# Seven products per gate/up side and per down projection: which PSUM bank each adds into, which engine reads it, and in what order

## The chip, the cores and the metric

One core of a Trainium2 chip runs the program. The time is device time in microseconds of one execution of the whole layer; the runs of before took 1701.79 us in the median of three (1700.83 to 1703.76). TensorE (PE) multiplies matrices and adds the results in PSUM; ScalarE (ACT), VectorE (DVE) and GpSimd (POOL) do elementwise work; SyncE (SP) issues the transfers. Each engine works through a queue of its own in order and waits there for what an instruction needs.

## What is computed

One layer of a sequence model for 1024 tokens of width 1024 in float32: a gated feed-forward network (FFN), a mixer (a gated convolution beside a state space model) and a second FFN. The changed code serves the two FFNs:

```python
def swiglu(h, w_gate, w_up, w_down):
    return (jax.nn.silu(h @ w_gate) * (h @ w_up)) @ w_down
...
h = modulate(rms_norm(x, ffn1_norm[l]), sh1, sc1)
x = x + 0.5 * g1[:, None, :] * swiglu(h, ffn1_w_gate[l], ffn1_w_up[l], ffn1_w_down[l])
```

The FFN is 2816 wide.

## The kernel before

**Products.** A float32 product is made of three matmuls (`mm3`): each operand is split into a high part of the type fp32r and a low part, and high x high, high x low and low x high are added up in PSUM. The FFN's width is cut into 11 groups of 256, called fa0 to fa10 in the first FFN and fb0 to fb10 in the second. In most of them (fa2 to fa10 and fb1 to fb10, 19 groups) gate and up are each a product of 2 x 2 blocks made of seven block products instead of eight (`seven`, from line 649). One block product is 12 matmuls. The blocks of the activations on the left are A11, A12, A22 and four combinations S1 to S4. The weights on the right have combinations as well: t1 to t4 beside chunks 0, 2 and 3. Each side, gate (g) and up (u), gives four results: (0,0), (0,1), (1,0) and (1,1). The results of gate pass through silu, those of up are multiplied by them. Most groups keep these products for the down projection (`keep`), and make their sums S1, S2, S3 (`keep_sums`) and S4 (`keep_last`) at once.

**Banks.** A product adds into a PSUM tile of its side: fa6gC is bank C of the gate side of group fa6. Before, the order on a side is A11 into A, S1 into C, S2 into B, S3 into D, A12 into A, A22 into E, S4 into C: five banks. ScalarE copies bank A after A11 (tile t, shown as fa6gt), before A12 adds to it. VectorE adds: u2 = t1 + B, u3 = u2 + D, t1 = u3 + C, u3 = u3 + E, u2 = u2 + C; u2 and u3 are shown as fa6gu. S4 adds to bank C after VectorE has read it for t1 = u3 + C.

**Down projections.** Four calls of `down7` (line 735), fad_0 and fad_1 in the first FFN (lines 1434 and on) and fbd_0 and fbd_1 in the second, use the same scheme with two pieces for each block product, in the order A11, S2, A12, S3, S1, A22, S4 (banks A, B, A, B, C, B, C). Each result goes into x with one VectorE operation (`update`).

**Weights.** The class `Weights` (line 121) feeds them. SyncE loads raw tiles (two slots). GpSimd makes f = chunk 2 - chunk 1 (line 168, in a tile `sums`, two slots) and t1 (line 169), later t2 = f + chunk 0 (line 177) and t4 = chunk 3 - t2 (line 179). ScalarE casts a chunk to the high part (CAST), VectorE subtracts for the low part. Two chunks make a granule, which serves two products; there are three slots `w` for granules.

**What sets the order.** The code calls the engines in the order of the products; side work (the rotors and tables of the state space model: `rott`, `kc`, `mi`, `rt`, `tab`, `kk`, `ph`, `pd`) is let in by a clock that counts products. But outside the first part of the program the framework's scheduler orders each engine's queue, so which instruction stands behind which is seen in the order of the built program, not in the code.

Of the kernel before, what the change touches and what calls it, by code (L numbers as in the profile page):

```python
# [13 lines left out]
F32 = mybir.dt.float32  # L14
# [7 lines left out]
P = 128  # L22
# [98 lines left out]
class Weights:  # L121
# [5 lines left out]
    SEVEN = (0, "t1", "t2", "t3", 3, "t4", 2)  # L127
    SECOND = (0, "t2", 3, "t3", "t1", "t4", 2)

    def __init__(self, engines, srcs, granules, raw_bufs):  # L130
# [4 lines left out]
        for pair in granules:  # L135
            for j, _ in pair:
                self.left[j] += 1
# [26 lines left out]
    def combine(self, j):  # L164
# [5 lines left out]
        self.sums[j] = {"t1": r[1], "t2": r[0], "t3": f, "t4": r[0]}  # L170

    def split_done(self, j, c):

        if j in self.combined and c in (0, "t2"):
            s, r = self.sums[j], self.raws[j][:, :HALF]
            if c == 0:
                self.G.tensor_tensor(out=r, in0=s["t3"], in1=r, op=ALU.add)  # L177
            else:
                self.G.tensor_tensor(out=r, in0=self.chunk(j, 3), in1=r, op=ALU.subtract)  # L179
# [6 lines left out]
    def pump(self):  # L186
        while self.slots and len(self.tiles) < len(self.granules):
# [22 lines left out]
            for j, _ in pair:  # L210
                self.left[j] -= 1
# [24 lines left out]
def hymba_layer(ctx: ExitStack, tc, x_d, xt_d, wm1_d, wmod_d, gu1_d, gs1_d, ds1_d, wl1_d, win_d, wout_d, glu_d, gu2_d, gs2_d, wd2_d, ds2_d, wl2_d, cols_d, cond_d, lam_d, bc_d, out_d):  # L236
# [54 lines left out]
    def stream(gu, gs, wd, ds, wl, m):  # L291
# [4 lines left out]
        for g in range(m, NGRP):  # L296
# [3 lines left out]
            seven = [(i, c) for i in (j, j + 1 + inner) for c in Weights.SEVEN]  # L300
# [5 lines left out]
        for c in range(CHUNKS):  # L306
            for p in range(2):
                j = len(srcs)
                srcs.extend([ds[c, p, 0], ds[c, p, 1]])
                granules.extend([(j, s), (j + 1, s)] for s in Weights.SECOND)  # L310
# [334 lines left out]

    SEVEN = (("A11", "A"), ("S1", "C"), ("S2", "B"), ("S3", "D"), ("A12", "A"), ("A22", "E"), ("S4", "C"))
    SECOND = (("A11", "A"), ("S2", "B"), ("A12", "A"), ("S3", "B"), ("S1", "C"), ("A22", "B"), ("S4", "C"))

    def seven(name, between, place=1, kept=None, then=None):


        a_tiles, gate_, taken = {}, {}, []

        for side in "gu":
            bank, res = {}, {}

            def add(dst, src, b):
                V.tensor_tensor(out=dst[:], in0=src[:], in1=bank[b][:], op=ALU.add)

            def out(h, fi, t):  # L660
                nm = f"{name}_{fi}_{h}"
                if side == "g":
                    A.activation(t[:], t[:], AF.Silu)
                    gate_[h, fi] = t
                elif kept is None:
                    V.tensor_tensor(out=t[:], in0=t[:], in1=gate_[h, fi][:], op=ALU.mult)
                    a_tiles[fi, h] = split_act(t[:], nm + "a")
                else:
                    keep(kept, f"A{h + 1}{fi + 1}", t[:], gate_[h, fi][:], ALU.mult, name, t[:])

            for n, (left, b) in enumerate(SEVEN):
                q = n + 7 * (side == "u")
                if q % 2 == 0:
                    taken = ws.take()
                opens = b not in bank
                if opens:
                    bank[b] = ps(f"{name}{side}{b}")
                for k in range(4):
                    while len(blocks[left]) <= k:
                        clock.step()  # L680
                    mm3(bank[b][:], taken[0], q % 2 * 4 + k, blocks[left][k], opens and k == 0, k == 3, more=not opens)
                nm = f"{name}{side}"
                if n == 0:
                    t1 = t2k(nm + "t1")
                    A.copy(t1[:], bank["A"][:])
                elif n == 2:
                    u2 = t2k(nm + "u2")
                    add(u2, t1, "B")
                elif n == 3:
                    u3 = t2k(nm + "u3")  # L690
                    add(u3, u2, "D")
# [1207 lines left out]
```

## Time and profile before

| | |
|---|---|
| time, median of three runs | 1701.79 us (1700.83 to 1703.76) |
| span of the profiled execution | 1704.7 us |
| mean granted TensorE clock | 0.994 |
| TensorE matmuls | 1666.8 us busy, 7545 instructions |
| VectorE | 1255.5 us busy |
| ScalarE | 630.1 us busy |
| GpSimd | 382.0 us busy |

The first FFN takes up about the first third of the span, the mixer the second, the second FFN the last. A profile row such as `fa2gC<-h1S,w` names the tile that is written and those that are read; `[0.93 <-DVE fa2gt]` behind a row is the time that the engine was idle just before it, and the engine and the tile that ended that. In a list of waits the columns are the total in us, how often, and the longest.

### The profile page before, as it was taken

What the parts mean: (1) busy time and instruction counts of PE and PEld (TensorE: products, weight loads), DVE (VectorE), ACT (ScalarE), POOL (GpSimd) and SP (SyncE); (2) the same over time, 40 slices, a digit from 0 to 9 for tenths busy, and PEclk for the clock granted to TensorE, in tenths of its full rate; (3) what the DMA queues carried; (4) which work ended last, traced back from release to release, by engine and by line L of the source; (5) the groups of instructions that cost most, each with busy time, mean ns of one, the idle gap of its engine ahead of it and who ended that gap; (6) DMA issues with size and microseconds to landing.
All of it is one profiled execution on the core that took longest, in us unless ns stands there. A gap on an engine that the chain in (4) does not pass through costs nothing.

```text
span 1704.7 us, 20844 instructions
## 1 busy us (share of the span) xinstructions
PE 1666.8 (98%) x7545; PEld 1369.9 (80%) x7545; DVE 1255.5 (74%) x1957; ACT 630.1 (37%) x1064; POOL 382.0 (22%) x297
## 2 busy tenths in 40 slices
PE   8999999999999999999999999999999999999997
PEld 5888877788878888788777878888888888888886
DVE  7897899998589978735555857957767667576655
ACT  6525323333354332331113415434344434322233
POOL 1012222242222412100000021122333223333212
PEclk9999999999999999999999999999999999999999
DMA  8544454544665448244654232324443343759212
GB/s 350 187 148 137 172 189 155 183 149 139 213 216 170 151 152 291 70 111 149 191 151 134 70 129 112 112 74 182 188 174 148 148 173 148 269 228 381 110 50 99
DMA packets 101625, 281.48 MB, mean 165 GB/s; under 512 B 19345, under 2 KB 34961, under 8 KB 90386
## 3 DMA queue, kind: packets, MB, share of 16 engines
q1 hardware_dynamic: 101522, 280.15, 46.6%
q8 instruction: 59, 0.97, 0.2%
q14 instruction: 44, 0.36, 0.1%
HBM read 195.69 MB, written 76.02 MB: 159 GB/s over the span
## 4 chain that ended last, share of the span: by engine, by line
PE 70%; DVE 8%; DMA 5%; issue 1%; ACT 0%; SPq 0%; POOL 0%; DVEq 0%; ACTq 0%; POOLq 0%
PE wo L112 4%; PE fald L112 3%; PE fb10d L112 2%; PE u L112 2%; PE fbd_1B L112 2%; PE fbd_0B L112 2%; DMA swz<-si 2%; DVE w L112 2%; PE fad_1B L112 2%; PE b L112 2%; PE fad_0B L112 1%; PE c L112 1%; PE fb0u L112 1%; PE fad_1C L112 1%; PE fbd_1C L112 1%; PE fbd_0C L112 1%
## 5 line engine op out<-in xcount | busy, mean ns | idle before, releaser
L112 ACT CAST w<-raw 128x512 fp32r<-128x512 f32 (+1 forms) x374 | 240.9, 677 | 497.7 <-issue 72.7
L112 DVE TENSOR_TENSOR w<-raw,w 128x512 fp32r<-128x512 f32 (+1 forms) x374 | 311.2, 851 | 101.2 <-ACT w L112 100.6
L177 POOL TENSOR_TENSOR raw<-sums,raw 128x512 f32<-128x512 f32 x54 | 81.6, 1511 | 420.9 <-DVE w L112 419.9
L168 POOL TENSOR_TENSOR sums<-raw 128x512 f32<-128x512 f32 x54 | 76.4, 1415 | 308.1 <-DMA raw<-in_ds 129.1
L179 POOL TENSOR_TENSOR raw<-raw 128x512 f32<-128x512 f32 x54 | 82.3, 1526 | 86.6 <-DVE w L112 86.0
L112 DVE CUSTOM_DVE_ANT_0 wm<-wm,cact 128x1024 f32<-128x1024 f32 x56 | 77.7, 1407 | 15.1 <-DMA wm<-in_wmod 15.0
L169 POOL TENSOR_TENSOR raw<-raw 128x512 f32<-128x512 f32 x54 | 85.2, 1577 | 4.2
L370 POOL TENSOR_TENSOR n3aq<-n3aq,n3aq 128x512 f32<-128x512 f32 x5 | 7.5, 1499 | 277.4 <-ACT n3aq L112 277.2
L112 DVE TENSOR_TENSOR w<-sums,w 128x512 fp32r<-128x512 f32 x54 | 54.9, 1029 | 3.4 <-ACT w L112 2.8
L112 PE MATMUL p<-h,w 128*128 128x512 f32 x192 | 49.4, 407 | 2.0 <-ACT h L112 1.5
L112 PE MATMUL wo<-oa,w 128*128 128x512 f32 x192 | 45.5, 391 | 2.1 <-ACT w L112 1.3
L112 PE MATMUL c<-h,w 128*128 128x512 f32 x192 | 47.1, 397 | 0.0
L112 PE MATMUL v<-h,w 128*128 128x512 f32 x192 | 46.9, 395 | 0.0
L112 PE MATMUL b<-h,w 128*128 128x512 f32 x192 | 45.6, 393 | 0.0
L112 PE MATMUL wo<-ob,w 128*128 128x512 f32 x192 | 45.2, 391 | 0.0
L112 PE MATMUL u<-h,w 128*128 128x512 f32 x192 | 44.8, 392 | 0.2 <-DVE h L112 0.2
L112 PEld LDWEIGHTS wo<-oa,w 128*128 128x128 f32 x192 | 35.8, 188 | 10.2 <-ACT w L112 1.7
L112 PEld LDWEIGHTS p<-h,w 128*128 128x128 f32 x192 | 35.7, 192 | 10.1 <-ACT h L112 2.0
L112 ACT CAST w<-sums 128x512 fp32r<-128x512 f32 x54 | 32.7, 619 | 28.8 <-PE fa10gE L112 2.5
L112 PEld LDWEIGHTS u<-h,w 128*128 128x128 f32 x192 | 35.7, 188 | 8.3 <-DVE h L112 0.6
L112 PEld LDWEIGHTS wo<-ob,w 128*128 128x128 f32 x192 | 35.8, 188 | 7.4
L112 PEld LDWEIGHTS c<-h,w 128*128 128x128 f32 x192 | 35.8, 190 | 7.2
(1579 smaller groups left out, 4039.8 us busy)
## 6 DMA issues: line engine op xcount, KB each, us to landing
raw<-in_gs SPq DMA_DIRECT2D x38, 1024.0 KB, 5.0
wm<-in_wmod SPq DMA_DIRECT2D x56, 512.0 KB, 5.2
raw<-in_ds SPq DMA_DIRECT2D x16, 1024.0 KB, 6.6
mw<-in_wm SPq DMA_DIRECT2D x8, 1024.0 KB, 8.4
raw<-in_win SPq DMA_DIRECT2D x8, 1024.0 KB, 5.5
raw<-in_gu SPq DMA_DIRECT2D x6, 1024.0 KB, 4.9
raw<-in_wl SPq DMA_DIRECT2D x5, 1024.0 KB, 6.7
xb<-in_xt SPq DMA_DIRECT2D x8, 512.0 KB, 6.4
```

The source lines that it names most:

```text
L112: r = getattr(self.engine, name)(*args, **kw)
L168: self.G.tensor_tensor(out=f, in0=r[2], in1=r[1], op=ALU.subtract)
L169: self.G.tensor_tensor(out=r[1], in0=r[1], in1=r[0], op=ALU.subtract)
L177: self.G.tensor_tensor(out=r, in0=s["t3"], in1=r, op=ALU.add)
L179: self.G.tensor_tensor(out=r, in0=self.chunk(j, 3), in1=r, op=ALU.subtract)
L370: nc.gpsimd.tensor_tensor(out=a, in0=a, in1=sq[:, :n], op=ALU.add)
```

## The change

Each side now has six products: A11 into B, S1 into C, S2 into B, A12 into A, S3 into B, S4 into C. Bank B carries A11, A11 + S2 and A11 + S2 + S3 in turn. ScalarE copies it after A11 (t1) and after S2 (u2), and copies bank C after S1 (c1). VectorE adds t1 + A for the result (0,0), c1 + B for (1,1) and u2 + C for (0,1). After both sides come the two A22 products, one adding to bank B of gate, one to bank B of up, and the result (1,0) is read straight from these banks. `down7` follows the same order, with A22 last. The granules of the weights follow: the two t4 form one at the group's end; t4 now lies in the tile `sums` instead of the raw tile, and a raw tile counts as free before t4 is used. `keep_sums` and `keep_last` both come behind the second A22. The tiles and products of the mixer stay as they were.

```diff
-    SEVEN = (0, "t1", "t2", "t3", 3, "t4", 2)
-    SECOND = (0, "t2", 3, "t3", "t1", "t4", 2)
+    SIX = (0, "t1", "t2", 3, "t3", 2)
+    ALL = (*SIX, "t4")
...
-            for j, _ in pair:
-                self.left[j] += 1
+            for j, c in pair:
+                self.left[j] += c != "t4"
...
-        self.sums[j] = {"t1": r[1], "t2": r[0], "t3": f, "t4": r[0]}
+        self.sums[j] = {"t1": r[1], "t2": r[0], "t3": f, "t4": f}
...
-        if j in self.combined and c in (0, "t2"):
-            s, r = self.sums[j], self.raws[j][:, :HALF]
+        if j in self.combined and c in (0, "t3"):
+            f, r = self.sums[j]["t3"], self.raws[j][:, :HALF]
             if c == 0:
-                self.G.tensor_tensor(out=r, in0=s["t3"], in1=r, op=ALU.add)
+                self.G.tensor_tensor(out=r, in0=f, in1=r, op=ALU.add)
             else:
-                self.G.tensor_tensor(out=r, in0=self.chunk(j, 3), in1=r, op=ALU.subtract)
+                self.G.tensor_tensor(out=f, in0=self.chunk(j, 3), in1=r, op=ALU.subtract)
...
-            for j, _ in pair:
-                self.left[j] -= 1
+            for j, c in pair:
+                self.left[j] -= c != "t4"
...
-            seven = [(i, c) for i in (j, j + 1 + inner) for c in Weights.SEVEN]
+            both = (j, j + 1 + inner)
+            seven = [(i, c) for i in both for c in Weights.SIX] + [(i, "t4") for i in both]
...
-                granules.extend([(j, s), (j + 1, s)] for s in Weights.SECOND)
+                granules.extend([(j, s), (j + 1, s)] for s in Weights.ALL)
...
-    SEVEN = (("A11", "A"), ("S1", "C"), ("S2", "B"), ("S3", "D"), ("A12", "A"), ("A22", "E"), ("S4", "C"))
-    SECOND = (("A11", "A"), ("S2", "B"), ("A12", "A"), ("S3", "B"), ("S1", "C"), ("A22", "B"), ("S4", "C"))
+    SIX = (("A11", "B"), ("S1", "C"), ("S2", "B"), ("A12", "A"), ("S3", "B"), ("S4", "C"))
+    ALL = (*SIX, ("A22", "B"))
...
+        def product(side, left, b, w, half):
...
+                mm3(bank[b][:], w, 4 * half + k, blocks[left][k], opens and k == 0, k == 3, more=not opens)
+
+        def copied(side, b, nm):
+            t = t2k(f"{name}{side}{nm}")
+            A.copy(t[:], banks[side][b][:])
+            return t
+
+        def add(side, dst, b):
+            V.tensor_tensor(out=dst[:], in0=dst[:], in1=banks[side][b][:], op=ALU.add)
+
+        def out(side, h, fi, src, t):
+            if side == "g":
+                A.activation(t[:], src[:], AF.Silu)
+                gate_[h, fi] = t
+            elif kept is None:
+                V.tensor_tensor(out=t[:], in0=src[:], in1=gate_[h, fi][:], op=ALU.mult)
+                a_tiles[fi, h] = split_act(t[:], f"{name}_{fi}_{h}a")
+            else:
+                keep(kept, f"A{h + 1}{fi + 1}", src[:], gate_[h, fi][:], ALU.mult, name, t[:])
...
+            for n, (left, b) in enumerate(SIX):
+                if n % 2 == 0:
+                    (w,) = ws.take()
+                product(side, left, b, w, n % 2)
+                if n == 0:
+                    t1 = copied(side, "B", "t1")
+                elif n == 1:
+                    c1 = copied(side, "C", "c1")
+                elif n == 2:
+                    u2 = copied(side, "B", "u2")
+                elif n == 3:
+                    add(side, t1, "A")
+                    out(side, 0, 0, t1, t1)
+                elif n == 4:
+                    add(side, c1, "B")
+                    out(side, 1, 1, c1, c1)
                 else:
...
-                if n == 0:
-                    t1 = t2k(nm + "t1")
-                    A.copy(t1[:], bank["A"][:])
-                elif n == 2:
-                    u2 = t2k(nm + "u2")
-                    add(u2, t1, "B")
-                elif n == 3:
-                    u3 = t2k(nm + "u3")
-                    add(u3, u2, "D")
-                    add(t1, u3, "C")
-                    out(1, 1, t1)
...
-                elif n == 5:
-                    add(u3, u3, "E")
-                    out(1, 0, u3)
-                    if side == "u" and kept is not None and kept.sums:
-                        keep_sums(kept, name)
-                elif n == 6:
-                    add(u2, u2, "C")
-                    out(0, 1, u2)
-                    if side == "u" and kept is not None and kept.sums:
-                        keep_last(kept, name)
-                if q % 2:
+                    add(side, u2, "C")
+                    out(side, 0, 1, u2, u2)
+                if n % 2:
                     ws.free()
...
+        (w,) = ws.take()
+        for half, side in enumerate("gu"):
+            product(side, "A22", "B", w, half)
+            if side == "g":
+                last = pools["first"].tile([P, HALF], F32, tag="first", name=f"{name}c21") if "first" in pools else acc_in_mov(f"{name}c21")
+            out(side, 1, 0, banks[side]["B"], last)
+        ws.free()
+        if kept is not None and kept.sums:
+            keep_sums(kept, name)
+            keep_last(kept, name)
+        if then is not None:
+            then("A22")
...
                     if n == 0:
-                        t1[i] = t2k(nm + "t1")
-                        A.copy(t1[i][:], bank["A", i][:])
+                        copied(t1, "B", i, "t1")
                     elif n == 1:
-                        u2[i] = t2k(nm + "u2")
-                        add(u2, t1, "B", i)
+                        copied(c1, "C", i, "c1")
                     elif n == 2:
-                        update(i, 0, 0, bank["A", i])
+                        copied(u2, "B", i, "u2")
...
-                        u3[i] = t2k(nm + "u3")
-                        add(u3, t1, "B", i)
+                        add(t1, "A", i)
+                        update(i, 0, 0, t1[i])
                     elif n == 4:
-                        add(u3, u3, "C", i)
-                        update(i, 1, 1, u3[i])
+                        add(c1, "B", i)
+                        update(i, 1, 1, c1[i])
                     elif n == 5:
-                        add(t1, t1, "B", i)
-                        update(i, 1, 0, t1[i])
+                        add(u2, "C", i)
+                        update(i, 0, 1, u2[i])
                     else:
-                        add(u2, u2, "C", i)
-                        update(i, 0, 1, u2[i])
+                        update(i, 1, 0, bank["B", i])
```

How the queue of ScalarE changes, at the places that the prediction speaks of (a number behind a name tells tiles apart). First around the start of fa2, where `fa2gt` is the copy after A11 and `kk`, `ph`, `r`, `rt` are side work. Before the change:

```order
L112 COPY fa2gt_1136<-fa2gA 128x512
L112 ACTIVATE kk<-ph 128x1056
L112 CAST w_1160<-raw_690 128x512
L112 CAST w_1160<-raw_803 128x512
L112 ACTIVATE ph<-ph 128x1056
L112 COPY rt_1571<-kk 64x512
```

The same place after the change:

```order
L112 COPY fa2gt_1138<-fa2gB 128x512
L112 ACTIVATE kk<-ph 128x1056
L112 COPY fa2gc_1159<-fa2gC 128x512
L112 CAST w_1164<-raw_803 128x512 x2
L112 ACTIVATE ph<-ph 128x1056
L112 COPY fa2gu_1187<-fa2gB 128x512
L112 ACTIVATE ph<-ph 128x1056
L112 COPY r_706<-rn 128x32
```

The copies gc and gu stand between pieces of the side work.

In the second FFN, ScalarE's queue where fb5 begins; `fb4S` and `fb4A` are the kept sums and products of the group before, cast for the down projection. Before the change:

```order
L112 COPY fb5gt_10250<-fb5gA 128x512
L112 CAST fb4S_10205<-fb4ut_10085 128x512
L112 CAST fb4A_10223<-fb4uu_10120 128x512
L112 CAST w_10268<-raw_9984 128x512
L112 CAST w_10268<-raw_10092 128x512
L112 CAST fb4S_10228<-fb4uu_10120 128x512
```

The same place after the change:

```order
L112 COPY fb5gt_10200<-fb5gB 128x512
L112 CAST fb4S_10168<-fb4uc_10038 128x512
L112 CAST fb4S_10173<-fb4c_10140 128x512
L112 COPY fb5gc_10215<-fb5gC 128x512
L112 CAST fb4S_10178<-fb4uc_10038 128x512
L112 CAST w_10220<-raw_10008 128x512 x2
L112 COPY fb5gu_10238<-fb5gB 128x512
L112 CAST fb4S_10183<-fb4uu_10057 128x512
L112 CAST w_10255<-raw_10008 128x512 x2
```

The copies gc and gu have come in, gu behind the cast of a sum and of two weights. At the end of fa10's up side, ScalarE's queue after the change, where `fa1lS` is cast from a loaded tile for the down projection:

```order
L112 COPY fa10ut_4018<-fa10uB 128x512
L112 COPY fa10uc_4049<-fa10uC 128x512
L112 CAST w_4051<-sums_3781 128x512
L112 CAST w_4051<-sums_3926 128x512
L112 CAST fa1lS_4056<-fa1lS_4056 128x512
L112 COPY fa10uu_4084<-fa10uB 128x512
```

There the copy `fa10uu` stands behind that cast.

## What I expect, before the run

> **What bounds the kernel now.** I read the page first: the span, and the busy time of each engine.
>
> ```profile
> span 1704.7 us, 20844 instructions
> PE 1666.8 (98%) x7545; PEld 1369.9 (80%) x7545; DVE 1255.5 (74%) x1957; ACT 630.1 (37%) x1064; POOL 382.0 (22%) x297
> ```
>
> TensorE works 1666.8 of 1704.7 us, so 37.9 us are all that it does not work. The change leaves its 7545 matmuls alone, so only those 37.9 us can shrink, or grow. The next view, the waits of TensorE (us in total, times, longest), says which of them lie in code that the change touches:
>
> ```profile
> PE fa4gC L112 <- DVE fa4gt L112: 1.6, 1, 1.6
> PE fa10uC L112 <- DVE fa10ut L112: 1.5, 1, 1.5
> PE fad_0A L112 <- DVE w L112: 1.5, 2, 0.8
> ...
> PE fa5gC L112 <- DVE fa5gt L112: 1.2, 1, 1.2
> ...
> PE fa2gC L112 <- DVE fa2gt L112: 0.9, 1, 0.9
> PE fa5uC L112 <- DVE fa5ut L112: 0.9, 1, 0.9
> ...
> PE fa6gC L112 <- DVE fa6gt L112: 0.7, 1, 0.7
> ...
> PE fad_0B L112 <- DVE fad_0u L112: 0.5, 1, 0.5
> ```
>
> Six waits are for the gate/up products (gC and uC: the bank of S1 and S4), three are in the first down projection, fad. They sum to 1.6 + 1.5 + 1.2 + 0.9 + 0.9 + 0.7 = 6.8 for gate/up and 1.5 + 0.5 = 2.0 for fad: 8.8 us. The six gate/up waits are one mechanism: S4 adds to bank C only after VectorE has read it for t1 = u3 + C, which stands behind two other additions, and A12 and A22, two products, are all the time for that. All other waits of the list are in stages that the change leaves as they are (the mixer, the norms). The windows say where it is tight:
>
> ```profile
> core 0: us, PE busy (x) PEld busy (x) DVE busy (x) ACT busy (x) POOL busy (x), PEclk, DMA share, GB/s
> 230.00:280.00 50.00, 47.94 (x220) 38.39 (x219) 46.08 (x71) 15.32 (x27) 17.11 (x11) 1.00 0.51 171
> 330.00:380.00 50.00, 50.00 (x232) 40.69 (x231) 45.73 (x72) 17.68 (x31) 15.12 (x10) 1.00 0.54 187
> ...
> 1250.00:1450.00 200.00, 200.00 (x884) 165.62 (x883) 143.83 (x211) 82.35 (x146) 62.32 (x44) 1.00 0.43 164
> ```
>
> In the first FFN VectorE works 46 of 50 us, and TensorE is idle for 2.06 of 50 in the first window, which is the 1.2 and 0.9 of fa5; in the second FFN 143.8 of 200, and there TensorE stands still nowhere. So **the most that can be won is 8.8 us, 0.5%**, and whatever a new wait costs comes off it. The durations that I shall need come from one product, one copy and one addition:
>
> ```profile
> 1224.32 2.88 PE L112 MATMUL fb4gA<-h,w 128*128 128x512 f32 x12
> 1227.04 2.88 PE L112 MATMUL fb4gC<-h3S,w 128*128 128x512 f32 x12
> ```
>
> ```profile
> L112 ACT COPY fbd_1t<-fbd_1A 128x512 f32<-128x512 f32 x4 | 2.4, 588 | 6.8 <-PE fbd_1A L112 6.8
> ```
>
> ```profile
> L112 DVE TENSOR_TENSOR fbd_1u<-fbd_1t,fbd_1B 128x512 f32<-128x512 f32 x8 | 5.5, 688 | 16.3 <-PE fbd_1B L112 16.3
> ```
>
> A product is 1227.04 - 1224.32 = 2.72 us; a ScalarE copy from a bank is 0.59, a VectorE addition from a bank 0.69.
>
> **The change, part by part.** *Work moved.* Each side of each of 19 groups has three copies instead of one and three additions instead of five; so has each of the 4 x 2 x 2 pieces of the down projections. ScalarE gets 2 x (38 + 16) = 108 copies, 108 x 0.59 = 64 us; VectorE loses 108 additions, 108 x 0.69 = 75 us. On engines at 37% and 74% that beside TensorE's work costs and gains nothing by itself; what counts is who is awaited when.
>
> *The wait that goes.* S4 into C now needs only the first copy of C (c1), made four products earlier, so VectorE no longer stands between two products of a side. The waits of fa4g, fa5g, fa5u, fa6g and fa10u go: -1.6 - 1.2 - 0.9 - 0.7 - 1.5 = -5.9. Next to be late after them would be the weights' low halves; they are earlier too, since VectorE has four additions fewer in a group. Of the 2.0 in fad, where VectorE catches up, I take half: -1.0 (bounds -2.0 and 0).
>
> *The waits that come.* Bank B carries A11, S2 and S3 in turn. S2 starts at the earliest one product (S1) after A11, S3 one product (A12) after S2. In these 2.72 us the copy must be issued and done: 0.59 and, by the start of such copies in the trace, some 0.2 after the product. Slack 1.9 us, **if ScalarE is not held at an earlier instruction**: its queue is in order. So I went through the new order of ScalarE group by group, and looked where something with a long wait or much work stands ahead of a copy. In the group A22 u needs bank B free of VectorE's c1 + B, with two products' time (5.44 us): slack over 3. In the down projections a product is two pieces, and the windows are twice 2.72 and more: 0.
>
> *fa2, where ScalarE is full.* TensorE's rows, then ScalarE's:
>
> ```profile
> 119.87 2.88 PE L112 MATMUL fa2gA<-h,w 128*128 128x512 f32 x12
> ...
> 130.75 2.88 PE L112 MATMUL fa2gA<-h,w 128*128 128x512 f32 x12
> ```
>
> ```profile
> 127.53 1.09 ACT L112 ACTIVATE kk<-ph 128x1056 f32<-128x1056 f32 x1 [4.15 <-DVE w L112]
> 128.52 1.12 ACT L112 CAST w<-raw 128x512 fp32r<-128x512 f32 x2
> 129.55 1.09 ACT L112 ACTIVATE ph<-ph 128x1056 f32<-128x1056 f32 x1
> ...
> 143.83 1.68 ACT L112 ACTIVATE tab<-pd 64x256 f32<-64x256 f32 x4
> 145.54 0.63 ACT L112 ACTIVATE fa2gu<-fa2gu 128x512 f32<-128x512 f32 x1
> 146.08 0.57 ACT L112 COPY fa2ut<-fa2uA 128x512 f32<-128x512 f32 x1
> ```
>
> In the new order the copy gu stands behind kk, gc, two casts and one ph: kk cannot start earlier, as it waits for VectorE. From 128.5: gc 0.58, casts 1.12, ph 1.1, gu 0.6, and 0.2 to be seen: 132.0. S3 is the fifth product, due where the second A began, at 130.75: +1.3. Then u: without A22 of g, S2 of u is due eight products after 119.87, at 119.87 + 8 x 2.72 + 1.3 = 142.9. ScalarE works without a gap until 146.08 now; to the copy ut it gains two copies (+1.2), loses one silu (-0.6) and three tab (3 x 0.42 = -1.3), which makes the end of ut about 146.08 - 0.7 + 0.6 + 0.2 = 146.1: +3.2. The old wait of fa2g goes (-0.9). Together **+3.6** (bounds +0.5, if the scattered pieces overlap better than one after the other, and +5).
>
> *fa6, behind a DMA.*
>
> ```profile
> 288.20 2.90 PE L112 MATMUL fa6gB<-h1S,w 128*128 128x512 f32 x12
> ...
> 293.66 2.88 PE L112 MATMUL fa6gA<-h,w 128*128 128x512 f32 x12
> ```
>
> ```profile
> 285.60 0.63 ACT L112 ACTIVATE rott<-rot 64x512 f32<-64x512 f32 x1 [3.11 <-DVE rot L112]
> ...
> 290.84 0.58 ACT L112 COPY kc<-kp 16x512 f32<-16x512 f32 x1 [4.00 <-DMA si_d<-rot]
> 291.32 0.57 ACT L112 COPY mi<-tp 128x512 f32<-128x512 f32 x1
> 291.92 1.14 ACT L112 CAST w<-raw 128x512 fp32r<-128x512 f32 x2
> ```
>
> The order now reads gt, rott, kc, mi, gc, two casts, gu. kc waits for a DMA that carries the rotors' result, 4.0 us here. From mi at 291.32: 0.6 for it, 0.6 for gc, 1.1 for the casts, 0.6 for gu and 0.2: about 294.3. S3 is due at 293.66, where the fifth product of the side began: +0.6; with the u side and fa7, which have the same rows a little better placed, **+0.8** (bounds 0 and +4.5, if rott itself comes later).
>
> *fa10u, behind a load.*
>
> ```profile
> 463.25 2.88 PE L112 MATMUL fa10uA<-h,w 128*128 128x512 f32 x12
> ```
>
> ```profile
> 469.64 0.62 ACT L112 CAST fa1lS<-fa1lS 128x512 fp32r<-128x512 f32 x1 [1.33 <-DMA fa1lS<-kept1Z]
> ```
>
> In the new order a cast of fa1lS, which waits for its load, stands just ahead of the copy uu. The u side starts one product earlier than now, at 460.53, and S3 is due at 460.53 + 4 x 2.72 = 471.4; the load came in at 469.6, and in the new order of SyncE's queue two more transfers stand ahead of it. I take **+1.0** (bounds 0 and +4).
>
> *The second FFN and the other groups.* Here the rows say 0. Products kept for later (keep_sums, keep_last) now both come after the last product, so VectorE does a tail of some ten operations while the next group's A11 and S1 run:
>
> ```profile
> 1221.49 1.78 DVE L112 TENSOR_TENSOR w<-sums,w 128x512 fp32r<-128x512 f32 x1
> 1223.20 0.67 DVE L112 TENSOR_TENSOR fb3uu<-fb3uu,fb3uE 128x512 f32<-128x512 f32 x1
> ...
> 1233.14 0.68 DVE L112 TENSOR_TENSOR fb3S<-fb3uu,fb3S 128x512 fp32r<-128x512 f32 x1
> ```
>
> ```profile
> 1229.96 1.14 ACT L112 CAST w<-raw 128x512 fp32r<-128x512 f32 x2
> ```
>
> Before, the tail from 1223.20 to 1233.82 was 10.6 us long and hurt nobody. Now the cast of fb4S, S2's, waits for the eighth operation of it, and the copy gu of fb5 stands behind that cast and two more. Take T as the end of A22 u: 0.9 for the first operation, 8 x 0.60, 0.6 + 1.1 + 0.6 on ScalarE and 0.2: T + 8.2; the product S2 ends at T + 8.2 anyway, so gu is done at T + 9.0. S3 is due at T + 10.9. A cast's low half at the time of a GpSimd operation takes 1.78 instead of 0.69, so three of them would make it T + 11.5: late by 0.6. By its queue GpSimd has one operation there, t4 of the next source, behind a low half of the tail; the combinations of the source after that stand ahead of it and wait for their load. With one hit gu is done at T + 9.3. I take 0, price if wrong 0.5 to 1.5 us in each of nine groups.
>
> *Weights.* t4 now lies in the sums tile and the raw tile is given back one granule (5.44 us) earlier, so loads start earlier; against that the next group's first combination on GpSimd must wait for t4's low half. It has two granules, 10.9 us, for two operations of 1.5 us and the split behind them: 0, and if it does not hold, it is part of the slower rival.
>
> **Sum:** -5.9 - 1.0 + 3.6 + 0.8 + 1.0 = **-1.5 us**. The profiled span would be 1704.7 - 1.5 = 1703.2; it stands 2.9 us (0.17%) above the median of the three runs, 1701.79, which I take as the profiling, so 1701.8 - 1.5 = **1700.3 us**. 0.2% is 3.4 us, about what a measurement of this kernel can tell from no change: the forecast lies within it.
>
> **The rivals.** *All waits go, no new one comes* (faster): ScalarE's copies slip in, because the pieces ahead of them are earlier as VectorE is lighter. Then -5.9 - 0.9 - 1.0 to -2.0: 1693 to 1694; with half of fa2's loss, 1696. For it: ScalarE at 37%, 17.7 of 50 us in the first FFN. Against: exactly at fa2 it works without a gap, and the copy of kc truly waited 4.0 us. *ScalarE's queue holds the copies back in every group* (slower): it decides once the eighth operation of VectorE's tail is later than T + 8.4, which takes three contended low halves. Nine groups at 0.5 to 1.5 us on the sum: 1700.3 + 4.5 to + 13.5, 1705 to 1714, likeliest near the lower end. For it: a row of 1.78 does stand at that place; against: GpSimd works 62 of 200 us there, and only one of its operations belongs there. *The change does not do what it says*: TensorE's new order shows the six products and the two A22 at the end, so I give this nothing.
>
> A rival of the clock: every window above grants 1.00, also the first, with 2.06 us of TensorE idle in it. If the new small waits on bank B made the clock fall to half for one product in each of 19 groups, that would be 19 x 2.72 = 52 us, 1752. The Trainium skill, "TensorE: Matmul & The Clock Gate", section "A second HAM failure mode: psum-queue depth-cycling", says that a TensorE that cycles through PSUM banks and idles briefly between groups of matmuls can have its clock swing; fewer banks in turn is such a change. This trace speaks against it here, with its 1.00 beside waits of that size.
>
> **How the numbers follow.** Forecast 0.42, within 0.2% of before (1698.4 to 1705.2). Faster rival 0.30, slower one 0.27, the clock 0.01. The range leaves out the last tenth on each side: 1693.5, all waits gone, to 1709, the slower rival at about 1 us a group. Faster 0.30, same 0.42, slower 0.28.
>
> **What would show it.** Right: no wait of TensorE on gt or ut of VectorE in fa4 to fa10; new ones on ScalarE's tiles at fa2 of about 1.3 and 3.2 us, at fa6 and fa10 under 2; 50.00 of 50 in the second FFN; ScalarE near 694 and VectorE near 1180 us busy. Wrong: a wait on a ScalarE copy in each of fb2 to fb10 (the slower rival), or none at fa2 (the faster one); raw tiles late, seen as waits on w.

## The result

The changed kernel takes **1715.03 us** in the median (1713.59 to 1717.26, four runs), the kernel before 1702.78 (1700.83 to 1705.9): a ratio of **1.0074, 95% interval 1.0058 to 1.0091**, 12.3 us slower. The forecast was 1700.3 us, and the time lies above the range that went with it.

### The profile page after: what moved, and what is told of

It reads as the page before. It is cut to its first block, busy times and chain, and to the rows that moved or that the text cites. A ratio compares the mean times of both kernels' runs of the same rounds, so it can differ in the third digit from the quotient of the medians.

```text
span 1715.5 us, 20814 instructions
## 1 busy us (share of the span) xinstructions
PE 1670.9 (97%) x7545; PEld 1373.1 (80%) x7545; DVE 1192.8 (70%) x1849; ACT 687.8 (40%) x1172; POOL 411.3 (24%) x297
## 4 chain that ended last, share of the span: by engine, by line
PE 50%; DVE 3%; DMA 3%; issue 0%; SPq 0%; ACT 0%; DVEq 0%; ACTq 0%
PE wo L112 4%; PE fbd_1B L112 3%; PE fbd_0B L112 3%; PE fb10d L112 2%; PE u L112 2%; DMA swz<-si 2%; PE b L112 2%; PE fb0u L112 1%; PE c L112 1%; PE fbd_1C L112 1%; PE fbd_0C L112 1%; PE fb0d L112 1%; PE fb0g L112 1%; PE gl L112 1%; PE v L112 1%; PE yy L112 1%
## 5 line engine op out<-in xcount | busy, mean ns | idle before, releaser
L112 DVE TENSOR_TENSOR w<-raw,w 128x512 fp32r<-128x512 f32 (+1 forms) x320 | 272.3, 869 | 92.8 <-ACT w L112 92.1
L112 ACT CAST w<-raw 128x512 fp32r<-128x512 f32 (+1 forms) x320 | 209.3, 687 | 289.6 <-POOL raw L177 37.4
L179 POOL TENSOR_TENSOR sums<-raw 128x512 f32<-128x512 f32 x54 | 98.7, 1834 | 464.3 <-DVE w L112 464.3
L168 POOL TENSOR_TENSOR sums<-raw 128x512 f32<-128x512 f32 x54 | 82.8, 1534 | 228.2 <-DVE w L112 109.0
L112 DVE TENSOR_TENSOR w<-sums,w 128x512 fp32r<-128x512 f32 x108 | 75.3, 718 | 87.1 <-ACT w L112 86.9
L177 POOL TENSOR_TENSOR raw<-sums,raw 128x512 f32<-128x512 f32 x54 | 91.5, 1697 | 131.5 <-DVE w L112 131.3
L112 ACT CAST w<-sums 128x512 fp32r<-128x512 f32 x108 | 63.7, 621 | 66.6 <-PE fbd_1A L112 15.5
L169 POOL TENSOR_TENSOR raw<-raw 128x512 f32<-128x512 f32 x54 | 82.2, 1522 | 4.2
L112 PEld LDWEIGHTS b<-h,w 128*128 128x128 f32 x192 | 35.5, 188 | 7.2
```

The source lines that it names most:

```text
L112: r = getattr(self.engine, name)(*args, **kw)
L168: self.G.tensor_tensor(out=f, in0=r[2], in1=r[1], op=ALU.subtract)
L169: self.G.tensor_tensor(out=r[1], in0=r[1], in1=r[0], op=ALU.subtract)
L177: self.G.tensor_tensor(out=r, in0=f, in1=r, op=ALU.add)
L179: self.G.tensor_tensor(out=f, in0=self.chunk(j, 3), in1=r, op=ALU.subtract)
```

## The profile after

The page's span and busy times:

```profile
span 1715.5 us, 20814 instructions
PE 1670.9 (97%) x7545; PEld 1373.1 (80%) x7545; DVE 1192.8 (70%) x1849; ACT 687.8 (40%) x1172; POOL 411.3 (24%) x297
```

The work moved as counted, 108 instructions out of VectorE and 108 into ScalarE: VectorE went from 1255.5 to 1192.8 us, ScalarE from 630.1 to 687.8. TensorE is 4 us busier with the same 7545 matmuls, and GpSimd 29 us busier with the same 297 instructions. Both are signs of the same instructions taking longer. The waits of TensorE (us in total, times, longest):

```profile
PE fa4uB L112 <- ACT fa4ut L112: 4.6, 1, 4.6
...
PE fa2uB L112 <- ACT fa2ut L112: 2.7, 1, 2.7
...
PE fa6uB L112 <- ACT fa6ut L112: 2.3, 1, 2.3
...
PE fa10uB L112 <- DVE fa10uc L112: 1.4, 1, 1.4
...
PE fa5uB L112 <- ACT fa5uu L112: 1.2, 1, 1.2
...
PE fa2gB L112 <- ACT fa2gu L112: 0.7, 1, 0.7
...
PE fa4uB L112 <- DVE fa4uc L112: 0.5, 1, 0.5
```

The old waits on gt and ut of VectorE are gone, as forecast. In their place stand waits of 2.3 to 4.6 us for the copy `ut`, ahead of S2 of the up side, in fa2, fa4 and fa6. The windows show one thing more, in the column ahead of the last two, the granted clock:

```profile
core 0: us, PE busy (x) PEld busy (x) DVE busy (x) ACT busy (x) POOL busy (x), PEclk, DMA share, GB/s
120.00:180.00 60.00, 56.59 (x236) 45.91 (x235) 39.07 (x83) 31.61 (x60) 17.16 (x10) 0.94 0.37 120
230.00:280.00 50.00, 48.99 (x216) 39.02 (x216) 43.15 (x67) 17.81 (x33) 18.09 (x11) 0.97 0.60 194
280.00:330.00 50.00, 45.21 (x195) 35.62 (x196) 39.97 (x63) 17.84 (x33) 17.91 (x10) 0.93 0.46 151
1250.00:1450.00 200.00, 200.00 (x884) 165.60 (x883) 134.62 (x186) 94.47 (x168) 64.41 (x42) 1.00 0.46 165
```

The clock is 0.94, 0.97 and 0.93 in the three windows that hold these waits and the work right behind them; it was 1.00 in the same three windows before. In the second FFN nothing is lost.

When each stage begins, by its first matmul, gives the ledger. These are the differences in a stage's length against the profile of before, in us, for the changed kernel and for the experiments that follow:

| stage | changed | down_only | seven_only | silu_later | filler | t4_dve | tail_waits | hybrid |
|---|---|---|---|---|---|---|---|---|
| fa2 | +5.65 | -0.55 | +4.36 | +6.30 | +2.89 | +3.14 | +3.42 | -0.28 |
| fa4 | +5.39 | +0.02 | +5.69 | +7.74 | +15.04 | +0.55 | +2.21 | +0.29 |
| fa5 | -1.17 | +0.29 | -1.43 | -2.28 | -1.90 | +1.25 | -1.20 | -1.01 |
| fa6 | +5.98 | -0.08 | +4.56 | +3.53 | +3.75 | -0.97 | +2.20 | +0.18 |
| fa7 | +0.50 | 0.00 | +1.66 | +1.37 | +1.95 | 0.00 | +0.76 | 0.00 |
| fad | -3.21 | -2.67 | -3.22 | -3.22 | -3.22 | -3.22 | -3.22 | -3.22 |
| fb1 to fbd | 0.00 | 0.00 | 0.00 | 0.00 | 0.00 | 0.00 | 0.00 | 0.00 |

For the changed kernel the other rows are +1.06 ahead of fa2, -0.1 for fa3 and fa8 to fa10 together, and -3.35 for the mixer. No instruction was changed or moved in the mixer, and yet it is shorter by 0.9 to 6.0 us in each of these profiles; so a single profile of it says nothing about the change, and I leave it out of the reading. A part of it is the clock: the profile before holds 10.2 us at a granted clock of 0.5 in the mixer, the profiles of this table 3.4 or 6.8 us.

**One wait, followed back.** The longest one, in fa4, has five links, each in its own view. TensorE's rows, with the idle time before an instruction and what ended it:

```profile
222.98 2.88 PE L112 MATMUL fa4uC<-h1S,w 128*128 128x512 f32 x12
230.42 4.61 PE L112 MATMUL fa4uB<-h1S,w 128*128 128x512 f32 x12 [4.56 <-ACT fa4ut L112]
234.86 2.92 PE L112 MATMUL fa4uA<-h,w 128*128 128x512 f32 x12
```

It waits 4.56 us for the copy ut, and then S2 takes 4.61 us instead of 2.88: that is the lower clock. ScalarE:

```profile
222.38 0.62 ACT L112 CAST w<-raw 128x512 fp32r<-128x512 f32 x1
229.26 0.63 ACT L112 ACTIVATE fa4gu<-fa4gu 128x512 f32<-128x512 f32 x1 [6.27 <-DVE fa4gu L112]
229.80 0.57 ACT L112 COPY fa4ut<-fa4uB 128x512 f32<-128x512 f32 x1
```

The copy is started at once when its turn comes; but ahead of it in the queue stands the silu of gu, and that waited 6.27 us for VectorE. VectorE:

```profile
220.62 0.68 DVE L112 TENSOR_TENSOR fa4gc<-fa4gc,fa4gB 128x512 f32<-128x512 f32 x1
227.39 1.23 DVE L112 CUSTOM_DVE_ANT_0 wm<-wm,cact 128x1024 f32<-128x1024 f32 x1 [6.10 <-DMA wm<-in_wmod]
...
228.54 0.68 DVE L112 TENSOR_TENSOR fa4gu<-fa4gu,fa4gC 128x512 f32<-128x512 f32 x1
```

The addition to gu stands behind `wm`, an operation of the side work that waited 6.10 us for its load. SyncE, which issues the loads:

```profile
208.43 0.33 SPq L112 DMA_DIRECT2D kept3Y<-fa3Y  x1
215.53 0.33 SPq L112 DMA_DIRECT2D raw<-in_gs  x1
215.95 0.38 SPq L112 DMA_DIRECT2D kept3Z<-fa3Z  x1
216.38 0.42 SPq L112 DMA_DIRECT2D kept3W<-fa3W  x1
216.90 1.59 SPq L112 DMA_DIRECT2D co_d<-rot  x2
...
219.87 9.11 SPq L112 DMA_DIRECT2D wm<-in_wmod  x3
```

```profile
SPq L112 <- POOL sums L179: 5.9, 1, 5.9
```

Nothing is issued between 208.43 and 215.53, and 5.9 us of that is a wait of the raw tile's load for `POOL sums L179`, which is t4. Then seven transfers come out in a heap, and the first wm only behind them. And GpSimd:

```profile
196.89 1.67 POOL L177 TENSOR_TENSOR raw<-sums,raw 128x512 f32<-128x512 f32 x1 [0.63 <-DVE w L112]
209.15 6.35 POOL L179 TENSOR_TENSOR sums<-raw 128x512 f32<-128x512 f32 x1 [10.59 <-DVE w L112]
216.13 1.67 POOL L177 TENSOR_TENSOR raw<-sums,raw 128x512 f32<-128x512 f32 x1 [0.63 <-DVE w L112]
```

t4 took 6.35 us, where the operations beside it take 1.67. What VectorE did in that time:

```profile
208.92 0.69 DVE L112 TENSOR_TENSOR w<-raw,w 128x512 fp32r<-128x512 f32 x1
209.52 0.69 DVE L112 TENSOR_TENSOR fa3Z<-fa3Y,fa3X 128x512 f32<-128x512 f32 x1
210.12 0.69 DVE L112 TENSOR_TENSOR fa3Z<-fa3X,fa3Y 128x512 f32<-128x512 f32 x1
...
212.53 0.69 DVE L112 TENSOR_TENSOR rot<-rot,rott 128x512 f32<-128x512 f32 x1
213.13 1.22 DVE L112 CUSTOM_DVE_ANT_0 wm<-wm,cact 128x1024 f32<-128x1024 f32 x1
```

It worked through the kept sums (fa3Z, fa3W) and rotors without a gap; all of these read two tiles in SBUF. At the start of fa6 and of fa7, t4 takes 4.62 and 4.63 us beside the same tail.

It does not go this way each time. At the start of fa5, where VectorE's kept sums come in the same order, first GpSimd and then VectorE:

```profile
255.22 1.61 POOL L179 TENSOR_TENSOR sums<-raw 128x512 f32<-128x512 f32 x1 [9.99 <-DVE w L112]
```

```profile
255.60 1.78 DVE L112 TENSOR_TENSOR fa4Z<-fa4Y,fa4X 128x512 f32<-128x512 f32 x1
```

There t4 takes 1.61 us, and it is VectorE's first kept sum that is held, 1.78 us instead of 0.69. Of the 18 t4 of fa2 to fa10, four took 3.48 to 6.35 us, one 2.21 and the others about 1.6. What decides which of the two engines is held, no run here shows.

## The experiments

Each was timed beside the kernel before on the same chip; the ratios are to it.

**Which half of the change.** One kernel has only the new down projections, one only the new gate/up products. The weights of the old half keep their old scheme. Against the kernel before, the first one has the new `down7` and, in the weights (the second one likewise, with the new `seven` and its sources in `late4`):

```diff
-                granules.extend([(j, s), (j + 1, s)] for s in Weights.SECOND)
+                granules.extend([(j, s), (j + 1, s)] for s in Weights.ALL)
+                late4.update((j, j + 1))
...
-        self.sums[j] = {"t1": r[1], "t2": r[0], "t3": f, "t4": r[0]}
+        self.sums[j] = {"t1": r[1], "t2": r[0], "t3": f, "t4": f if j in late4 else r[0]}
```

> The gate/up products as before, the down projections (and their weights, with t4 in the sums tile) as changed. The changed kernel gained 3.2 us on before between the start of fad and the end of fald, and lost 17.3 us before that. Theory A (the loss sits in the gate/up products alone, the gain in the down projections is theirs): 1702.8 - 3 = about 1699.5 us, ratio 0.998, granted clock 1.00 throughout the first FFN. Rival B (the loss is t4 in the sums tile and GpSimd, the gain in fad only a recovery of what fa lost): 1703 to 1705.

Measured: 1700.91 us, ratio 0.9985 (0.9974 to 0.9995), as theory A has it: no loss in the first FFN, 2.67 us gained in fad. The run cannot part the gate/up products from their weights, though, since both keep the old scheme here.

> The gate/up products as changed, the down projections as before. Theory A: the loss is all there and the gain of 3.2 us is missing: about 1718 us, ratio 1.009 to 1.010, waits of TensorE on fa2ut, fa4ut, fa6ut of ScalarE with a lower clock behind each. Rival B (the loss needs both parts, because the queues of both meet): under 1712.

Measured: 1714.9 us, ratio 1.0070 (1.0057 to 1.0083), between the two numbers. The waits are there (4.4, 2.6 and 2.2 us), so the loss belongs to the gate/up half, to its products or to its weights. What I had wrong was the gain in fad: this kernel has the old down projections and gains 3.22 us there all the same. The two gains do not add up. My reading, not tested further, is that either half spares VectorE the backlog with which it entered fad.

**The silu ahead of the copy.** The first theory took the queue of ScalarE for the cause. In this kernel the silus of gate's results (1,1) and (0,1) are kept in a list and called only behind the up side's third copy.

```diff
+                if n == 2 and side == "u":
+                    u2 = copied(side, "B", "u2")
+                    copy = A.last
+                    for late in held:
+                        out("g", *late)
+                        A.follow(A.last, copy)
...
+                    if side == "g":
+                        held.append((1, 1, c1, c1))
...
+                    if side == "g":
+                        held.append((0, 1, u2, u2))
```

> The changed kernel, but the silu of gate's results (1,1) and (0,1) stands behind the up side's three copies in ScalarE's queue, so that the copy ut no longer waits for VectorE's additions. Theory A (copy ut of fa4 and fa6 was late only because of the silu ahead of it, which waited for VectorE, which waited for a DMA): waits on fa4ut and fa6ut under 0.5 us, clock 1.00 at fa4 and fa6, fa2 as it was: 1715.0 - 5 (fa4) - 5 (fa6) = about 1705 us, ratio 1.001. Rival C (the additions themselves are late, and the next product that needs one waits as long): above 1711, with waits of 2 to 5 us on uu or on VectorE's tiles in the same groups.

Measured: 1716.45 us, ratio 1.0078 (1.0064 to 1.0093): no gain. Rival C is right. TensorE's rows in fa4:

```profile
225.27 2.88 PE L112 MATMUL fa4uB<-h1S,w 128*128 128x512 f32 x12
...
232.37 3.04 PE L112 MATMUL fa4uB<-h1S,w 128*128 128x512 f32 x12 [1.49 <-ACT fa4uu L112]
...
245.98 5.39 PE L112 MATMUL fa4uB<-h,w 128*128 128x512 f32 x12 [5.14 <-DVE fa4uc L112]
```

S2 starts without a wait now; but S3 waits 1.49 us, and the last product waits 5.14 us for VectorE's addition to uc. The silu only handed on a lateness that came from VectorE, so the copy's place was not the root.

**The clock.** Is the lower clock a consequence of the waits, and what does it cost? I filled three waits with matmuls that nobody needs.

```diff
+                if side == "u" and n == 2 and name in FILL:
+                    idle = ps(f"{name}idle")
+                    ah = blocks["S1"][0][0]
+                    for _ in range(FILL[name]):
+                        T.matmul(idle[:], lhsT=ah[:, :P], rhs=ah, start=True, stop=True)
```

> The changed kernel, with 10, 18 and 9 matmuls into a spare bank ahead of S2 of the up side in fa2, fa4 and fa6, about 2.3, 4.1 and 2.0 us of work, where TensorE waited 2.7, 4.6 and 2.3 us. They add work and shorten no wait. Theory D (each of these waits is followed by a stretch at half clock that costs more: 3.1 us in fa2, 1.7 in fa4, 2.9 in fa6): clock 1.00 there and 1715.0 - 7.5 = about 1707.5 us, ratio 1.003. Rival E (the lower clock is not the waits' doing): 1715 or up to 2 us more, clock 0.5 to 0.66 behind the same places.

Measured: 1721.47 us, ratio 1.0108 (1.0093 to 1.0122): as a whole neither theory's number. In fa2 it did what was meant. TensorE's rows there, of the changed kernel and then with the filler:

```profile
146.54 5.49 PE L112 MATMUL fa2uB<-h1S,w 128*128 128x512 f32 x12 [2.67 <-ACT fa2ut L112]
151.83 3.31 PE L112 MATMUL fa2uA<-h,w 128*128 128x512 f32 x12
```

```profile
142.64 2.43 PE L112 MATMUL fa2idle<-h1S 128*128 128x512 f32 x10
145.44 3.06 PE L112 MATMUL fa2uB<-h1S,w 128*128 128x512 f32 x12 [0.37 <-ACT fa2ut L112]
148.33 2.88 PE L112 MATMUL fa2uA<-h,w 128*128 128x512 f32 x12
```

The wait of 2.67 us became 2.4 us of work and 0.37 of wait, S2 and A12 take 3.06 and 2.88 instead of 5.49 and 3.31, and the group is 2.8 us shorter, though S2 starts no earlier: 5.5 us after S1 in both kernels. In fa4 the filler did harm, +15.04 against +5.39: 4.1 us of it came on top of a wait that only moved on to the last product (6.4 us for uc), since the root there is elsewhere. So the run says something about the clock in fa2 and fa6 alone: it stayed at 1.00 in both (fa6 lost 3.75 us instead of 5.98), where the changed kernel had 6.8 us at 0.5 in each. What of the 2.8 us in fa2 is the filling's doing stays open, because chance has a part in it: other kernels whose wait of 2.4 to 2.6 us in fa2 was not filled lost 3.14 (t4_dve), 3.42 (tail_waits) and 3.16 us (dose_kept, below), hardly more than the 2.89 here. Their stretch at 0.5 was 3.4 us long, or did not come (dose_kept). To see the clock by itself, the copy ut was repeated in the second FFN, where nothing else waits.

```diff
+            for _ in range(DOSE.get(name, 1) if (side, nm) == ("u", "t1") else 1):
+                A.copy(t[:], banks[side][b][:])
```

> The changed kernel, with the copy ut repeated 8, 10, 12 and 16 times in fb3, fb5, fb7 and fb9, where TensorE now waits nowhere. At 0.55 us each, waits of TensorE of about 1.9, 3.0, 4.1 and 6.3 us, 15 us in all. Theory D (a long wait lowers the clock behind it, a short one does not): fb3 loses its wait alone, the three others 1.7 to 3.4 us more than their waits, clock 0.5 behind them: 1715 + 15 + 5 to 10 = 1735 to 1740 us. Rival E (the waits alone): 1730 us, clock 1.00.

Measured, in two runs: 1718.28 us, ratio 1.0089 (1.0068 to 1.0109). Neither, because the waits did not come about: the scheduler knew of the longer copies and put A12 ahead of S2. The trace shows waits of 0.5 us at most in these groups. The next kernel holds the products in their order: the first matmul of each product must follow the last one of the product before.

```diff
+                if name in DOSE and ends:
+                    A.follow(r0, ends[-1])
+                ends.append(r1)
```

> As dose, with the up side's products held in their order, and 6, 6, 7, 7, 8, 8, 10, 10 copies of ut in fb2 to fb9: waits of TensorE of about 1.5, 1.5, 2.6, 2.6, 3.7, 3.7, 4.8, 4.8 us, 25 us in all. Theory D: at 1.5 us the wait alone; at 2.6 and above up to 3.4 us at half clock behind the wait, 1.7 us lost each time, in six groups 6 to 12 us: 1746 to 1752 us. Rival E (the waits alone): 1740 us, clock 1.00.

Measured, in two runs: 1750.27 us, ratio 1.0282 (1.0256 to 1.0308), theory D's number. S2 of the up side in fb2, fb4, fb5, fb6, fb7, fb8 and fb9, with the waits of 1.4 to 4.7 us:

```profile
1180.46 3.02 PE L112 MATMUL fb2uB<-h3S,w 128*128 128x512 f32 x12 [1.42 <-ACT fb2ut L112]
...
1261.05 4.61 PE L112 MATMUL fb4uB<-h3S,w 128*128 128x512 f32 x12 [2.42 <-ACT fb4ut L112]
...
1303.46 3.06 PE L112 MATMUL fb5uB<-h3S,w 128*128 128x512 f32 x12 [2.42 <-ACT fb5ut L112]
...
1345.30 4.48 PE L112 MATMUL fb6uB<-h3S,w 128*128 128x512 f32 x12 [3.42 <-ACT fb6ut L112]
...
1388.72 5.49 PE L112 MATMUL fb7uB<-h3S,w 128*128 128x512 f32 x12 [3.42 <-ACT fb7ut L112]
...
1434.38 4.99 PE L112 MATMUL fb8uB<-h3S,w 128*128 128x512 f32 x12 [4.66 <-ACT fb8ut L112]
...
1479.39 4.61 PE L112 MATMUL fb9uB<-h3S,w 128*128 128x512 f32 x12 [4.66 <-ACT fb9ut L112]
```

Twelve matmuls take 3.0 us behind a wait of 1.42, and 4.5 to 5.5 behind waits of 3.42 and 4.66; at 2.42 one time 4.61 and one time 3.06. What the groups lost beyond the wait itself: 0.3 us in fb2 and fb3; 1.9 and 0.3 in fb4 and fb5; 1.9, 2.9, 2.3 and 1.9 in fb6 to fb9. So a wait of some 2.4 us may cost half clock and one of 3.4 us did each time, about 2 us on top. The other traces put the lower end further down. Counting the waits of TensorE in the two FFNs from fa2 on, in all the profiles of this case, 11 of 16 waits of 1.8 to 2.9 us were followed or overlapped by a stretch at a granted clock of 0.5, the shortest of them 1.78 us (filler, fa4) and 1.96 us (t4_dve, fa5); so were all 11 waits of 3.0 us and more, and no wait of 0.9 to 1.7 us set one off. A stretch there lasts 3.4 us or two or three times that, never anything between; at half clock each 3.4 us can cost up to half of it, 1.7 us. The Trainium skill, "TensorE: Matmul & The Clock Gate", section "What's actually happening", says that after at least one idle window of about 3.4 us, which runs free of the program, the clock drops to half, and that it takes about as long in work to come back. The drop to half agrees, and so does the length of a stretch; the waits of 1.8 to 2.4 us that already met it are shorter than that window.

**GpSimd's t4.** The chain above ends at an operation that takes four times as long as it should. First, VectorE makes t4 itself.

```diff
-                self.G.tensor_tensor(out=f, in0=self.chunk(j, 3), in1=r, op=ALU.subtract)
+                self.V.tensor_tensor(out=f, in0=self.chunk(j, 3), in1=r, op=ALU.subtract)
```

> The changed kernel, but VectorE, not GpSimd, makes t4 from chunk 3 and t2. Theory F (in fa4 and fa6 the root is GpSimd's t4: it takes 6.35 and 4.62 us instead of about 1.5 while VectorE works through the kept sums without a gap, the raw tile's next load waits for it, and behind that load SyncE's queue holds back the loads and stores of the side work, for which VectorE then waits ahead of its additions): no wait of TensorE over 1 us in fa4 and fa6, VectorE's waits for wm and si_d there under 2 us, fa2 as it was: 1715.0 - 5 to -11 = 1704 to 1710 us, ratio 1.001 to 1.004. Rival G (the loads come late for another reason, and VectorE has 54 more operations, 37 us): 1714 to 1718 us.

Measured: **1701.49 us, ratio 0.9993 (0.9981 to 1.0004)**, 13.5 us below the changed kernel and better than I had expected; its interval takes in 1, so it cannot be told from the kernel before. One line carries most of the loss. SyncE's rows at fa4:

```profile
206.48 0.33 SPq L112 DMA_DIRECT2D raw<-in_gs  x1
...
213.62 7.68 SPq L112 DMA_DIRECT2D wm<-in_wmod  x3
```

Counted from fa4's first matmul (at 200.22 here, at 203.94 in the changed kernel), the raw tile's load goes out after 6.3 us instead of 11.6, and the first wm after 13.4 instead of 15.9. fa4 loses 0.55 us, fa6 gains 0.97. fa5 loses 1.25: it waits 1.96 us for the copy uu, with half clock behind. fa2 keeps its wait of 2.4 us, but loses 3.14 instead of 5.65, as the stretch at half clock is shorter there and the wait on gu is gone; that part of the 13.5 us is not shown to be t4's doing. VectorE's wait for wm in fa4 is still 2.8 us, more than I had expected, and harmless.

Then the same with GpSimd keeping t4, but VectorE made to wait for it, after fa3, fa5 and fa6:

```diff
+        if name in ("fa3", "fa5", "fa6"):
+            info = mybir.DependencyInfo(mybir.DependencyClass.Sync, mybir.DependencyReason.DATA)
+            tc.add_manual_dep(V.last.ins, ws.last_t4.ins.name, info, reason="t4 first")
```

> The changed kernel with one wait more: after fa3, fa5 and fa6 VectorE's second kept sum waits until GpSimd has made t4 of the next group. GpSimd keeps all its work. Theory H (GpSimd's t4 was not slow by itself or for want of data, but because VectorE's back-to-back operations with two inputs in SBUF kept it out): t4 there 2.5 us or less instead of 6.35, 4.62 and 4.63, the raw load behind it some 4 us earlier, waits of TensorE on fa4ut and fa6ut under 1.5 us: 1715.0 - 5 to -11 = 1704 to 1710 us. Rival I (t4 is late because of what it waits for, and moving it to VectorE helped by shortening the hand-over): VectorE only loses time, 1714 to 1718 us.

Measured: 1708.01 us, ratio 1.0030 (1.0017 to 1.0043). Theory H holds. GpSimd's t4 at fa4:

```profile
205.72 2.21 POOL L179 TENSOR_TENSOR sums<-raw 128x512 f32<-128x512 f32 x1 [10.59 <-DVE w L112]
```

And VectorE's kept sum that now waits for it:

```profile
207.97 0.69 DVE L112 TENSOR_TENSOR fa3Z<-fa3Y,fa3X 128x512 f32<-128x512 f32 x1 [1.18 <-POOL sums L179]
```

t4 takes 2.21 us instead of 6.35, by a wait added to another engine, and the kernel is 7 us faster for it. The raw tile's load goes out 7.4 us after fa4's first matmul instead of 11.6, and the waits on fa4ut and fa6ut are gone. It is not as good as moving t4, and VectorE's pause may be why: a wait of 1.9 us on fa4gu is new. The Trainium skill, "SBUF — State Buffer", section "Who interferes with whom", says that a VectorE instruction with two SBUF inputs contends with a GpSimd instruction that reads SBUF, and that contention for what the two engines share is an exclusive lock. The 6.35 us beside VectorE's row of such instructions agree, and so do the 1.78 us of VectorE at the start of fa5. No experiment here varies the kind of VectorE work beside t4, so that it takes two SBUF inputs is not shown by these runs alone.

**Putting it together.** fa2 keeps its old products and banks, all else is as changed, with t4 on VectorE.

```diff
+    def seven_any(name, *args, **kw):
+        return (seven if name in AS_BEFORE else seven_six)(name, *args, **kw)
...
+            if m == SEVEN_FROM[0] and f"fa{g}" in AS_BEFORE:
+                seven = [(i, c) for i in both for c in Weights.SEVEN]
```

> fa2 as before the change, all other groups and the down projections as changed, t4 of these on VectorE. Theory F with theory A for fa2 (ScalarE's side work there fills its queue): 0 in fa2, 0 to -6 in fa3 to fa10, -3 in the down projections: 1694 to 1700 us, ratio 0.995 to 0.9985, the fastest so far. If fa4 and fa6 keep their waits (rival G): 1704 to 1710 us.

Measured: **1699.56 us, ratio 0.9980 (0.9971 to 0.9989)**, the lowest median of all. Its interval overlaps that of down_only, which has no new gate/up product at all, so the two cannot be told apart. fa2 is at -0.28: its loss came with the new order and leaves with it. Of the gain, 3.22 us lie in fad; fa2 to fa10 together are 0.9 us shorter than before. So once the harm is removed, the new order of the gate/up products by itself wins about 1 us in this one profile. What is left are waits of 0.7 to 1.4 us in fa2, fa4, fa5, fa6 and fa10.

## Why the prediction was wrong

- *What bounds the kernel* (8.8 us at most to be won): the right waits, but too low a bound. fad was given 2.0 us at most and gained 3.2; a short wait costs about 0.3 us beyond itself (dose_kept), and fad had three. The best version wins about 3 us, all told.
- *The profiled span*, 2.9 us above the median, "which I take as the profiling": a wrong reading without effect on the difference. In the changed kernel the profiled run's time is 1717.26 us and its span 1715.5, so the span lies below the time. The profiled execution before was a longer one, with its 10.2 us at half clock in the mixer.
- *Work moved, and the old wait that goes*: right. No wait on VectorE's gt or ut is left; fa5 gained 1.17 of the 2.1, since a copy uu is 1.2 us late there.
- *fa2, +3.6*: the right engine and mechanism, a sum of the wrong terms. The waits were 0.73 and 2.67 instead of 1.3 and 3.2, and the 3.2 us beyond them, up to +5.65, I had not in the sum: nearly all of it the clock (S2 and A12 alone are 3.0 us longer). I gave a falling clock one chance in a hundred because windows with two waits of about 1 us still showed 1.00. The same sum forecast a wait of 3.2 us, longer than any in that row, and I did not ask what the clock does there. The rival of the clock had it fall in each of 19 groups behind small waits; it fell in three, behind the long ones.
- *Weights, 0*: **this is the step that failed**. I gave the next combination, which waits for t4's low half, "two granules, 10.9 us, for two operations of 1.5 us". The duration was that of GpSimd undisturbed, and the step asked only when the weights are ready. It did not ask who else waits for t4: the raw tile's next load, since t4 is the last to read the tile, and in SyncE's queue everything behind that load. I had even named the tail of VectorE and the contention with GpSimd, but only for what it does to VectorE (the row of 1.78), not for what it does to GpSimd. The sign that I named, "raw tiles late, seen as waits on w", did not show it either: the raw tile was late, but TensorE's waits stood on the copies. t4_dve and tail_waits show the size of this term: from fa4 to fa7, 9.9 us and 6.7 us come back.
- *fa4, -1.6, and fa6, +0.1*: wrong by that same chain, +5.39 and +5.98. The prediction named no new wait in fa4, and in fa6 it went through the rows ahead of the copies of gate. The silu ahead of ut, 0.63 us long, is in neither, nor is what that silu waits for.
- *fa10u, +1.0 for -1.5*: the stage came out at -0.1. A wait of 1.4 us is there, but for VectorE's addition before A22, not for the load. To this addition, c1 + B, the prediction gave a slack of over 3 us; fa4 waits 0.5 us for the same one.
- *fad, -1.0*: measured -3.21, outside its bounds of -2.0 and 0, and nearly as much from either half alone.
- *The second FFN, 0*: right, to a hundredth. The slower rival placed its loss there, at the tail of VectorE in every group. The tail did make the loss, but in the first FFN, through GpSimd. In the second, t4 of the gate/up weights takes 1.60 to 1.67 us each time, so there it is not held at all; why not stays open. The rival had the sign, not the mechanism.

What stays open: which share of the loss in fa6 is the clock's (a wait for VectorE's `bl` lies beside it), what decides whether GpSimd or VectorE is held, and what besides the clock makes the mixer shorter in these profiles.

## What to carry to other kernels

When a buffer is freed by another engine than before, follow the new releaser to everything queued behind the transfer that waits for it, and price the releaser at its contended duration, not at its mean. In this kernel a wait of TensorE of 3 us or more should be counted with some 2 us more for the clock, and one of about 2 to 3 us with a good chance of it, so avoiding one long wait is worth more than avoiding short ones of the same sum. And where a wait sits at the end of a queue, remove it at its root: moving the silu out of the way changed only the name of the wait.

## What I had not expected of the hardware

GpSimd's 128x512 subtraction took 6.35 us beside an unbroken row of VectorE operations with two SBUF inputs, and 2.21 us when VectorE paused once; beside the same row in another group it was VectorE that was held, 1.78 us instead of 0.69. The clock fell behind a single wait of 2.42 us (fb4) and even of 1.96 us (fa5 of t4_dve), though not behind the other of 2.42 us (fb5), and behind neither of 1.42 us. And each short wait cost about 0.3 us beyond itself (1.71 us lost for 1.42 waited).
